# A decoder block on one NeuronCore: seven products of quarters also for the six gate segments and the way out, and one list of steps

## The chip, the core and the metric

The kernel runs on one core of a Trainium2 chip. The metric is the device time of one execution in microseconds; before the change the median of three runs is 2732.26 us (2726.07 to 2732.51).

## What is computed

The input `x` has 2048 tokens of 1024 columns, all in float32; there is one layer.

```python
h = rms_norm(x, norm_mix)
c_gate, b_gate, a_in, u, v, g_a, g_b = split(h @ w_in)      # w_in: 1024 x 7168, seven segments of 1024
y_a = b_gate * causal_depthwise_conv3(c_gate * a_in)
y_b = gelu(u) * (tril(W_s[head]) @ layer_norm(gelu(v)) + b) # within chunks of 128 tokens, 8 heads
merged = sigmoid(g_a) * y_a + sigmoid(g_b) * y_b
x = x + merged @ w_out                                      # 1024 x 1024
hid = square(relu(rms_norm(x, norm_mlp) @ w_ff1))           # 1024 x 4096
x = x + hid @ w_ff2                                         # 4096 x 1024
return rms_norm(x, final_norm)
```

## The kernel before, in words

Every float32 operand of a product is split into two fp32r parts (`split`, lines 105 to 107): ScalarE copies the high part, VectorE subtracts it to get the low one. A product of two such pairs is three matmuls on TensorE, high by high, high by low and low by high (`mm3`, lines 109 to 113; `passes`, line 684 for the feed-forward part). One matmul takes a 128 x 128 stationary tile and 512 moving columns and adds into one of eight PSUM banks.

The tokens come in two blocks of 1024. Each block goes through the mixer: the `v` segment (`v_half`, with the layer norm in `layer_norm` and the products with `W_s` in `sgu_mix`, lines 372 and 373), then the six segments C, A, B, U, GA, GB for each group of 128 columns (`turned_half`), and the way out (`out_pass`, by `natural_pass`; line 592 adds the products to the rows of x). These use plain products, all eight steps over the 1024 rows of the weights. The mixer keeps its operands in 36 slots of 128 x 1024 (`big`).

The feed-forward part is cut otherwise. The activations (tokens by columns) and the weights are each seen as four quarters, and sums of quarters make seven products of half size in each direction instead of eight. The products have names, 1 to 7, and run in the order of `ORDER`, "1627543". FF1 (`ff1_steps`) makes a step of each product of a pair of column tiles: 12 matmuls on one bank. The steps of neighbouring pairs are interleaved. FF2 (`ff2_steps`) makes a step of each row tile of a product: 12 matmuls over four banks, and eight such steps follow one another before the next product begins. Sums of quarters of the activations are made once and kept in HBM (`h2d`, `hidd`; `quarter_jobs` makes those of `h2d`: it loads rows of x1, normalizes them, turns them on TensorE at line 394 and sums them); sums of the weights are made on VectorE just before use (line 674 subtracts, line 671 adds), and the result is split (`split_new`).

In "1627543" the products 1 and 2 share a bank or set of banks, 6, 7 and 4 a second and 5 and 3 a third, so that two products on one set never follow one another directly, except within FF1's interleaving. A product's first use of a bank clears it and later ones add to it, and between them VectorE or ScalarE reads it.

`drive` (line 693) writes the order: before it runs step s it issues the loads of steps up to s + 8 (9 in FF2), and makes the operands (`prep`) of steps up to s + 4. TensorE and SyncE (SP, the queue of the loads) keep the order in which the program is written; the other engines' order is planned by priority, and loaded x rows and splits in the mixer carry a raised priority (`PRIO`). The feed-forward part has 5 buffers for split weights (`wunit`), 12 for raw loads (`rawq`) and 7 for held operands (`hold`). Between the mixer and the feed-forward part the pools are closed and others opened. GpSimd (POOL) computes the power -0.5 of the norms and issues the DMAs that write `x1d`, `h2d` and `hidd`.

Of the kernel before, what the change touches and what calls it, by code (L numbers as in the profile page):

```python
# [8 lines left out]
F32 = mybir.dt.float32  # L9
# [12 lines left out]
PRIO = 600  # L22
# [3 lines left out]
ORDER = "1627543"  # L26
C_SEG, B_SEG, A_SEG, U_SEG, V_SEG, GA_SEG, GB_SEG = range(7)


@with_exitstack  # L30
def hybrid_block_kernel(
# [29 lines left out]

    nc = tc.nc
# [4 lines left out]
    H = sgu_w.shape[1]  # L67

    const = ctx.enter_context(tc.tile_pool(name="const", bufs=1))
    stat = ctx.enter_context(tc.tile_pool(name="stat", bufs=8))  # L70
    psum = ctx.enter_context(tc.tile_pool(name="psum", bufs=8, space=bass.MemoryType.PSUM))
    mixer = ctx.enter_context(ExitStack())

    def mixer_pool(name, bufs):
        return mixer.enter_context(tc.tile_pool(name=name, bufs=bufs, reuse_waits="tile"))

    mconst = mixer_pool("mconst", 1)
    big = mixer_pool("big", 36)
    rawp = mixer_pool("rawp", 3)
    hlp = mixer_pool("hlp", 3)  # L80
    work = mixer_pool("work", 4)
    bcp = mixer_pool("bcp", 3)
# [10 lines left out]
    def pair(t):  # L93
        return t.rearrange("p (a b) -> p a b", a=2)
# [4 lines left out]
    def wk():  # L99
        return work.tile([P, HB], F32, tag="wk", name=nm("wk"))  # L100

# [3 lines left out]
    def split(hi, lo, src):  # L105
        nc.scalar.activation(hi, src, AF.Copy)  # L106
        nc.vector.tensor_tensor(lo, src, hi.bitcast(F32), ALU.subtract)  # L107

    def mm3(ps, stat_hl, mov_hl, first, last):
        (sh, sl), (mh, ml) = stat_hl, mov_hl  # L110
        nc.tensor.matmul(ps, lhsT=sh, rhs=mh, start=first, stop=False)  # L111
        nc.tensor.matmul(ps, lhsT=sh, rhs=ml, start=False, stop=False)  # L112
        nc.tensor.matmul(ps, lhsT=sl, rhs=mh, start=False, stop=last)  # L113


    def nat(w, r0, c0):
        return w[r0 : r0 + 2 * P, c0 : c0 + HB].rearrange("(k p) c -> p k c", p=P)

    def trn(w, c0):
        return w[:, c0 : c0 + P].rearrange("(k p) c -> p k c", p=P)  # L120

    def j_order(j):
        if j % 2 == 0:
            return (C_SEG, A_SEG, B_SEG, U_SEG, GA_SEG, GB_SEG)
        return (C_SEG, A_SEG, B_SEG, GA_SEG, GB_SEG, U_SEG)

    ORDER_AB = ((0, 0), (0, 1), (1, 0), (1, 1))

    def block_units():
        u = []  # L130
        for hf, h in ORDER_AB:
            u += [(("v", hf, h, q), nat(w_in, 2 * P * q, V_SEG * D + h * HB)) for q in range(4)]
        for j in range(KT):
            u += [(("in", seg, j), trn(w_in, seg * D + j * P)) for seg in j_order(j)]
        for hf, h in ORDER_AB:
            u += [(("o", hf, h, q), nat(w_out, 2 * P * q, h * HB)) for q in range(4)]
        return u

    units = [u for _ in range(NBLK) for u in block_units()]
    raws, hls = {}, {}  # L140
    loaded, ready, used = [0], [0], [0]

    def load_to(n):
        while loaded[0] < min(n, len(units)):
            i = loaded[0]
            t = rawp.tile([P, D], F32, tag="raw", name=nm("raw"))
            src = units[i][1]
            nc.sync.dma_start(out=t.rearrange("p (k c) -> p k c", k=src.shape[1]), in_=src)
            raws[i] = t
            loaded[0] += 1  # L150

    def ready_to(n):
        while ready[0] < min(n, len(units)):
            i = ready[0]
            load_to(i + 1)
            t = hlp.tile([P, 2, D], F32R, tag="hl", name=nm("hl"))
            with tc.high_priority(offset=PRIO):
                split(t[:, 0, :], t[:, 1, :], raws.pop(i))
            hls[i] = t
            ready[0] += 1  # L160

    def unit(key, ahead=2):

        i = used[0]
        assert units[i][0] == key, (units[i][0], key)
        used[0] += 1
        ready_to(i + 1 + ahead)
        load_to(i + 6)
        t = hls.pop(i)
        k = units[i][1].shape[1]  # L170
        return [
            (
                t[:, 0, :].rearrange("p (k c) -> p k c", k=k)[:, m, :],
                t[:, 1, :].rearrange("p (k c) -> p k c", k=k)[:, m, :],
            )
            for m in range(k)
        ]
# [4 lines left out]
    mhalf = const.tile([P, CH], F32, name="mhalf")  # L182
    nc.gpsimd.memset(mhalf, -0.5)
    junk = const.tile([P, D], BF16, name="junk")
    vecs = const.tile([P, 5 * KT], F32, name="vecs")
    sguT = mconst.tile([P, H, 2, P], F32R, name="sguT")
    zt = mconst.tile([P, 2 + BLK], F32, name="zt")
    tails = mconst.tile([P, KT, 2], F32, name="tails")


    x1d = [[tc.dram_tile([P, D], F32, name=f"x1d{b}_{i}") for i in range(2 * CH)] for b in range(NBLK)]
    h2d = [{p: tc.dram_tile([P, CH, HB], F32, name=f"h2d{b}_{p}") for p in ORDER} for b in range(NBLK)]
    hidd = [{p: tc.dram_tile([P, NPAIR, HB], F32, name=f"hidd{b}_{p}") for p in ORDER} for b in range(NBLK)]

    def vec(row, k):
        return vecs[:, row * KT + k : row * KT + k + 1]

# [841 lines left out]
```

## Time and profile before

| what | value |
|---|---|
| median of three runs | 2732.26 us |
| the profiled execution: time, span | 2727.57 us, 2725.9 us |
| TensorE busy (PE) | 2688.8 us, 99% |
| VectorE busy (DVE) | 1529.3 us, 56% |
| ScalarE busy (ACT) | 1035.4 us, 38% |
| GpSimd busy (POOL) | 205.3 us, 8% |
| mean granted TensorE clock | 0.995 of full |
| moved by DMA | 354.45 MB |

The profiled execution is one run; its span goes from the first to the last instruction. Busy time is the union of an engine's instructions, so that in a group of matmuls that overlap in the pipeline the mean duration is longer than the distance from one to the next.

### The profile page before, as it was taken

The numbers are of one execution on the slowest core, as the hardware profiler recorded it, in microseconds if no ns is written. First come the engines' busy times: TensorE is split into PE (matmuls) and PEld (weight loads), VectorE is DVE, ScalarE is ACT, GpSimd is POOL, SyncE is SP. The second block draws the span as 40 slices with busy tenths as digits, with TensorE's granted clock in tenths as the row PEclk, the third lists the DMA queues.
The fourth block names the chain that finished last, engine by engine and source line by source line (L and its number), as shares of the span: only waits on it lengthen the run. The fifth ranks groups of instructions, "written<-read, shape, count | busy, mean of one in ns | idle before, by whom it ended". The sixth has DMA issues, their size and how long they took to land.

```text
span 2725.9 us, 31946 instructions
## 1 busy us (share of the span) xinstructions
PE 2688.8 (99%) x12061; PEld 2231.1 (82%) x12061; DVE 1529.3 (56%) x2336; ACT 1035.4 (38%) x1668; POOL 205.3 (8%) x381
## 2 busy tenths in 40 slices
PE   9999999999999999999998999999999999999998
PEld 7888888888888888888876888878888888888886
DVE  5752233223456322232356877686667779686885
ACT  5422222222343121222223555565555444464444
POOL 0000000000000000000021323212122000010001
PEclk9999999999999999999998999999999999999999
DMA  5211111113631111111267756474446654482631
GB/s 198 73 45 48 47 47 54 47 47 132 218 115 55 39 55 47 47 48 53 67 254 250 230 198 207 159 247 155 143 166 241 234 183 140 139 296 95 215 108 62
DMA packets 275166, 354.45 MB, mean 130 GB/s; under 512 B 16540, under 2 KB 181444, under 8 KB 275012
## 3 DMA queue, kind: packets, MB, share of 16 engines
q1 hardware_dynamic: 245700, 262.21, 29.9%
q0 software_dynamic: 24704, 81.81, 8.0%
q10 hardware_dynamic: 4608, 8.39, 0.8%
q8 instruction: 95, 1.56, 0.2%
q14 instruction: 59, 0.48, 0.1%
HBM read 262.16 MB, written 90.18 MB: 129 GB/s over the span
## 4 chain that ended last, share of the span: by engine, by line
PE 95%; DMA 2%; issue 1%; DVE 1%; ACT 0%; POOL 0%; SPq 0%; POOLq 0%; ACTq 0%; DVEq 0%
PE ps L684 43%; PE ps L113 17%; PE ps L111 17%; PE ps L112 16%; DMA rq<-h2d 1%; PE ps L373 1%; PE ps L372 1%; DMA big<-x1d 1%; PE ps L267 1%; PE ps L394 0%; PE ps L453 0%; DVE hold L107 0%; DMA rq<-in_w_ff_dram 0%; ACT hold L106 0%; DVE r L671 0%
## 5 line engine op out<-in xcount | busy, mean ns | idle before, releaser
L684 PE MATMUL ps<-hold,wu 128*128 128x512 f32 x2688 | 617.7, 392 | 16.0 <-ACT wu L106 10.2
L684 PEld LDWEIGHTS ps<-hold,wu 128*128 128x128 f32 x2688 | 507.6, 189 | 124.4 <-ACT wu L106 10.6
L684 PE MATMUL ps<-wu,hold 128*128 128x512 f32 x2688 | 609.4, 389 | 0.0
L111 PE MATMUL ps<-big,hl 128*128 128x512 f32 x1536 | 597.7, 389 | 0.0
L113 PE MATMUL ps<-big,hl 128*128 128x512 f32 x1536 | 597.6, 389 | 0.0
L112 PE MATMUL ps<-big,hl 128*128 128x512 f32 x1536 | 597.6, 389 | 0.0
L684 PEld LDWEIGHTS ps<-wu,hold 128*128 128x128 f32 x2688 | 504.5, 188 | 104.8
L106 ACT ACTIVATE hl<-raw 128x1024 fp32r<-128x1024 f32 x160 | 169.5, 1060 | 707.8 <-PE ps L113 575.4
L107 DVE TENSOR_TENSOR hl<-raw,hl 128x1024 fp32r<-128x1024 f32 x160 | 195.7, 1223 | 388.7 <-ACT hl L106 388.4
L113 PEld LDWEIGHTS ps<-big,hl 128*128 128x128 f32 x1536 | 288.3, 188 | 60.0
L112 PEld LDWEIGHTS ps<-big,hl 128*128 128x128 f32 x1536 | 288.4, 188 | 59.8
L111 PEld LDWEIGHTS ps<-big,hl 128*128 128x128 f32 x1536 | 288.3, 188 | 59.3
L111 PE MATMUL ps<-hl,big 128*128 128x512 f32 x512 | 200.4, 391 | 0.0
L113 PE MATMUL ps<-hl,big 128*128 128x512 f32 x512 | 199.4, 389 | 0.0
L112 PE MATMUL ps<-hl,big 128*128 128x512 f32 x512 | 199.2, 389 | 0.0
L107 DVE TENSOR_TENSOR hold<-rq,hold 128x512 fp32r<-128x512 f32 x280 | 181.5, 683 | 11.3 <-ACT hold L106 11.2
L106 ACT ACTIVATE hold<-rq 128x512 fp32r<-128x512 f32 x280 | 157.7, 618 | 54.7 <-DMA rq<-h2d 38.7
L106 ACT ACTIVATE wu<-hold 128x512 fp32r<-128x512 f32 x160 | 100.1, 629 | 193.8 <-PE ps L684 192.0
L107 DVE TENSOR_TENSOR wu<-hold,wu 128x512 fp32r<-128x512 f32 x160 | 109.7, 688 | 102.0 <-ACT wu L106 101.9
L802 POOL DMA_DIRECT2D hidd<-r x224 | 122.0, 545 | 467.3 <-ACT r L749 294.0
L106 ACT ACTIVATE wu<-rq 128x512 fp32r<-128x512 f32 x160 | 100.1, 628 | 117.9 <-PE ps L684 117.5
L107 DVE TENSOR_TENSOR wu<-rq,wu 128x512 fp32r<-128x512 f32 x160 | 109.7, 687 | 56.5 <-ACT wu L106 56.5
(120 smaller groups left out, 2150.3 us busy)
## 6 DMA issues: line engine op xcount, KB each, us to landing
raw<-in_w_in_dram SPq DMA_DIRECT2D x128, 512.0 KB, 3.7
hidd<-r POOLq DMA_DIRECT2D x224, 256.0 KB, 2.8
rq<-hidd SPq DMA_DIRECT2D x224, 256.0 KB, 3.5
rq<-in_w_ff_dram SPq DMA_DIRECT2D x128, 256.0 KB, 3.1
hold<-in_w_ff_dram SPq DMA_DIRECT2D x64, 512.0 KB, 7.4
big<-in_x_dram SPq DMA_DIRECT2D x32, 512.0 KB, 8.0
raw<-in_w_out_dram SPq DMA_DIRECT2D x32, 512.0 KB, 3.4
rq<-h2d SPq DMA_DIRECT2D x56, 256.0 KB, 5.1
```

Source lines behind the costliest of these rows:

```text
L106: nc.scalar.activation(hi, src, AF.Copy)
L107: nc.vector.tensor_tensor(lo, src, hi.bitcast(F32), ALU.subtract)
L111: nc.tensor.matmul(ps, lhsT=sh, rhs=mh, start=first, stop=False)
L112: nc.tensor.matmul(ps, lhsT=sh, rhs=ml, start=False, stop=False)
L113: nc.tensor.matmul(ps, lhsT=sl, rhs=mh, start=False, stop=last)
L267: nc.tensor.transpose(ps[:, i * P : (i + 1) * P], t[:, k * P : (k + 1) * P], ident)
L372: nc.tensor.matmul(o, lhsT=hi[:, cs], rhs=r, start=True, stop=False)
L373: nc.tensor.matmul(o, lhsT=lo[:, cs], rhs=r, start=False, stop=True)
L684: nc.tensor.matmul(ps, lhsT=stat_of(a), rhs=mov_of(b), start=first and n == 0, stop=last and n == 2, skip_group_check=goes_on,)
L802: nc.gpsimd.dma_start(out=hidd[blk][p2][:, i, :], in_=src)
```

## The change

The way of the feed-forward part is taken to the six gate segments and to the way out, whose 5376 matmuls become 4704; the `v` segment keeps plain products. The mixer's own helpers (`unit`, `natural_pass`, `turned_half`, `mm3`) go. Every stage is now a list of steps, and one `drive` runs the ten stages v0, in0, v1, in1, out0, out1, FF1 (two blocks) and FF2 (two blocks) with loads 8 steps and operands 3 steps ahead. What passes between stages lies in HBM: the sums of the normalized x of the second block (`h1d`), the mixed heads (`mixd`, written in pieces of 128 x 128), the sums of the merged rows (`md`) beside those that were there. The new order "1674253" lets 1, 6, 7 and 4 add up in one bank, with a reading after each. The layer norm and the products with `W_s` go in between the steps as jobs, row by row, and so do the jobs that make sums of quarters. The gain and bias of the layer norm move behind the products with `W_s`; the bias takes 16 matmuls of 256 columns. One set of pools serves all stages; raised priorities are dropped.

```diff
-ORDER = "1627543"
+ORDER = "1674253"
+GROUP = {"1": "b", "6": "b", "7": "b", "4": "b", "2": "d", "5": "c", "3": "c"}
...
-    big = mixer_pool("big", 36)
-    rawp = mixer_pool("rawp", 3)
-    hlp = mixer_pool("hlp", 3)
...
+    hold = pool("hold", 1)
+    wunit = pool("wunit", 4)
+    rawq = pool("rawq", 9)
+    half = pool("half", 8)
+    big = pool("big", 12)
...
+    def pair_steps(hq, cols, sink):
...
+        def run(p):
+            first = p in "125"
+            if first:
+                st[GROUP[p]] = bank()
+            ps = st[GROUP[p]]
+            u, h = units.pop(p), hq[p]
+            for k in range(CH):
+                passes(
+                    ps,
+                    lambda a: u[:, a, k * P : (k + 1) * P],
+                    lambda b: h[:, b, k, :],
+                    first and k == 0,
+                    k == CH - 1,
+                    not first,
+                )
+            if p in "167":
+                st["s" + p] = hf()
+                copy(st["s" + p], ps)
+            else:
+                m, n = QUARTER[p]
+                sink(m, n, ps, {"2": st["s1"], "3": st["s6"], "5": st["s7"], "4": None}[p])
...
+        for i in range(CH):
+            jobs += [lambda i=i: norm(i), nothing, lambda i=i: mix(i, 0), lambda i=i: mix(i, 1)]
...
+            def b_sink(m, n, ps, a, st=st):
+                y = st["y"][n][:, tok(m)]
+                mul(y, y, plus(hf() if a is not None else None, ps, a))
...
+    def row_steps(a_src, w, rows_of, nk, i0, x1, places, finish):
...
             for r in range(CH):
                 passes(
-                    banks[group][r],
+                    banks[GROUP[p]][r],
                     lambda a: h[:, a, n % CH, r * P : (r + 1) * P],
                     lambda b: u[:, b, :],
                     first and n == 0,
-                    n == NK - 1,
+                    n == nk - 1,
                     not first,
                 )
-            if n < NK - 1:
+            if n < nk - 1:
                 return
             for r in range(CH):
...
+                m, c = {"1": (0, 0), "6": (0, 1), "7": (1, 1)}.get(p) or QUARTER[p]
+                t = x1[r + m * CH][:, c * HB : (c + 1) * HB]
+                add(t, banks[GROUP[p]][r], t)
+                if p not in "167":
+                    finish(r + m * CH, c)
...
+        spread(v, 17, 0.9, 16, lambda blk=blk: late[blk, 0])
+        spread(inn, 0, 0.8, 16, lambda blk=blk: late[blk, 1])
...
+    jobs = h2_jobs(0)
+    spread(outs[1], 1, 0.8, len(jobs), lambda jobs=jobs: jobs)
+    jobs2 = h2_jobs(1)
+    spread(ff1s[0], 16, 4, len(jobs2), lambda: jobs2)
+    for ph in outs + ff1s + [ff2_steps(blk, rotate("453")) for blk in blocks]:
+        phases += ph
...
+    drive(phases, 8, 3)
```

`spread(steps, n0, every, ...)` puts job i in front of step `int(n0 + i * every)`. The jobs of one row pair in `h2_jobs` are, in this order, load and normalize row r, turn it, load and normalize row r + 4, turn it, sum. `late[blk, m]` holds for each of four rows the norm, an empty job and two jobs of products with `W_s`.

## Rows read from the trace of the kernel before

**Rows 1.** Page, part 1: busy time, share of the span, instructions.

```profile
PE 2688.8 (99%) x12061; PEld 2231.1 (82%) x12061; DVE 1529.3 (56%) x2336; ACT 1035.4 (38%) x1668; POOL 205.3 (8%) x381
```

**Rows 2.** Page, part 4: the chain that ended last, by engine.

```profile
PE 95%; DMA 2%; issue 1%; DVE 1%; ACT 0%; POOL 0%; SPq 0%; POOLq 0%; ACTq 0%; DVEq 0%
```

**Rows 3.** Windows of start, FF1, FF2 and end: length, busy us (instructions) by engine, clock, DMA.

```profile
0.00:13.00 13.00, 8.93 (x27) 6.58 (x28) 4.52 (x11) 6.94 (x10) 3.38 (x14) 1.00 0.86 330
...
1810.00:2040.00 230.00, 230.00 (x1016) 190.41 (x1016) 159.50 (x251) 118.69 (x197) 45.40 (x84) 1.00 0.49 160
2101.00:2711.00 610.00, 610.00 (x2693) 505.11 (x2692) 473.29 (x800) 285.19 (x523) 15.04 (x18) 1.00 0.49 169
2711.00:2726.00 15.00, 1.83 (x9) 1.18 (x7) 7.10 (x16) 5.78 (x12) 3.65 (x4) 0.73 0.37 140
```

**Rows 4.** Timeline of PE where stages meet: start, us, work, idle before it.

```profile
1373.61 3.27 PE L394 MATMUL ps<-ident,big 128*128 128x128 f32 x16 [3.98 <-DVE st L249]
...
1474.04 5.20 PE L684 MATMUL ps<-hold,wu 128*128 128x512 f32 x12 [10.21 <-ACT wu L106]
...
1481.26 12.81 PE L684 MATMUL ps<-hold,wu 128*128 128x512 f32 x48 [0.55 <-DVE hold L107]
1494.86 5.52 PE L684 MATMUL ps<-hold,wu 128*128 128x512 f32 x23 [0.80 <-DVE hold L107]
...
1799.56 3.02 PE L684 MATMUL ps<-hold,wu 128*128 128x512 f32 x12 [0.88 <-ACT h L771]
1805.16 7.13 PE L684 MATMUL ps<-hold,wu 128*128 128x512 f32 x23 [2.58 <-DVE h L671]
```

**Rows 5.** Page, part 5: matmul groups of the mixer's three passes, one of each shape.

```profile
L111 PE MATMUL ps<-big,hl 128*128 128x512 f32 x1536 | 597.7, 389 | 0.0
...
L111 PE MATMUL ps<-hl,big 128*128 128x512 f32 x512 | 200.4, 391 | 0.0
```

**Rows 6.** The chain in order of time: start, us, what.

```profile
1524.87 1.75 PE ps L394 x16
1526.61 54.43 PE ps L684 x240
```

**Rows 7.** Groups by line and shape: count, busy us, mean ns of one, idle before.

```profile
L107 DVE TENSOR_TENSOR hold<-rq,hold 128x512 fp32r<-128x512 f32 x280 | 181.5, 683 | 11.3 <-ACT hold L106 11.2
L106 ACT ACTIVATE wu<-hold 128x512 fp32r<-128x512 f32 x160 | 100.1, 629 | 193.8 <-PE ps L684 192.0 <-DMA out_dram<-r 0.8 <-ACT r L991 0.7
...
L373 PE MATMUL ps<-sguT,big 128*128 128x256 f32 x128 | 31.2, 281 | 0.0
...
L107 DVE TENSOR_TENSOR big<-big,big 128x1024 fp32r<-128x1024 f32 x16 | 19.5, 1220 | 2.3 <-ACT big L106 2.3
...
L225 DVE TENSOR_TENSOR big<-big,wk 128x128 f32<-128x128 f32 x8 | 1.8, 282 | 0.0
```

**Rows 8.** Timeline of DVE in FF2: end of product 6, end of product 7.

```profile
2148.12 2.48 DVE L671 TENSOR_TENSOR r<-ps,r 128x512 f32<-128x512 f32 x4
...
2188.58 0.69 DVE L107 TENSOR_TENSOR wu<-hold,wu 128x512 fp32r<-128x512 f32 x1 [2.03 <-ACT wu L106]
2189.19 2.48 DVE L671 TENSOR_TENSOR r<-ps,r 128x512 f32<-128x512 f32 x4
```

**Rows 9.** DMAs: one chain piece (start, us), then issues: count, KB each, us to landing.

```profile
1462.25 3.06 DMA x1d<-big
...
x1d<-big POOLq DMA_DIRECT2D x16, 512.0 KB, 10.2
...
jr<-x1d SPq DMA_DIRECT2D x8, 512.0 KB, 5.9
```

**Rows 10.** Windows of 2 us after idle times, columns as in rows 3.

```profile
1474.00:1476.00 2.00, 1.96 (x5) 1.54 (x6) 1.41 (x3) 0.00 (x0) 0.00 (x0) 0.50 1.10 323
...
1798.00:1800.00 2.00, 1.12 (x6) 0.62 (x5) 1.97 (x4) 1.61 (x3) 1.08 (x2) 1.00 0.92 273
...
1806.00:1808.00 2.00, 2.00 (x7) 1.62 (x6) 2.00 (x4) 2.00 (x5) 0.00 (x0) 0.61 0.76 260
```

More of the change, by code (lines that the diff above doesn't have):

```diff
@@ L21 @@
 CH = HB // P
-PRIO = 600
 WARM = 20
@@ L139, in hybrid_block_kernel @@
[L139 to L174, printed above, removed]
-            )
-            for m in range(k)
-        ]
+    def held(place, dt=F32R):
+        shape = [P, 2, CH, HB] if dt == F32R else [P, CH, D]
+        return hold.tile(shape, dt, tag=f"hold{place}", name=nm("hold"))
@@ new lines, in add, with sub, mul, copy @@
+    def add(o, a, b):
+        nc.vector.tensor_tensor(o, a, b, ALU.add)
+    def sub(o, a, b):
+        nc.vector.tensor_tensor(o, a, b, ALU.subtract)
+    def mul(o, a, b):
+        nc.vector.tensor_tensor(o, a, b, ALU.mult)
+    def copy(o, a):
+        nc.scalar.activation(o, a, AF.Copy)
+    def split(h, l, src):
+        copy(h, src)
+        sub(l, src, h.bitcast(F32))
+    def split_new(src):
+        u = wtile()
+        split(u[:, 0, :], u[:, 1, :], src)
+        return u
+    def passes(ps, stat_of, mov_of, first, last, goes_on=False):
+        for n, (a, b) in enumerate(((0, 0), (0, 1), (1, 0))):
+            nc.tensor.matmul(
+                ps,
+                lhsT=stat_of(a),
+                rhs=mov_of(b),
+                start=first and n == 0,
+                stop=last and n == 2,
+                skip_group_check=goes_on,
+            )
@@ new lines, in quarters, with load, prep @@
+    def quarters(hq, src, p, place=None):
+        parts = []
+        def load():
+            for r in range(CH):
+                t = rq()
+                nc.sync.dma_start(out=t, in_=src[p][:, r, :])
+                parts.append(t)
+        def prep():
+            t = held(place or p)
+            for r, part in enumerate(parts):
+                tr = slice(r * P, (r + 1) * P)
+                split(t[:, 0, :, tr], t[:, 1, :, tr], part.rearrange("p (k t) -> p k t", k=CH))
+            hq[p] = t
+        return load, prep
@@ L209, in load_sgu, with stagger, plus @@
+    def stagger(pairs):
+        place = {}
+        for i, pr in enumerate(pairs):
+            for n, p in enumerate(ORDER):
+                place[7 * i + 2 * n + 1] = pr[p]
+        return [place[k] for k in sorted(place)]
+    def plus(t, ps, addend):
+        if addend is None:
+            return ps
+        add(t, ps, addend)
+        return t
+    sg = {}
     def load_sgu():
@@ L975, in finish, with ff2_steps @@
+    def ff2_steps(blk, nxt):
+        x1, fs = [None] * (2 * CH), {}
+        sums = {}
+        def finish(i, h):
+            if not sums:
+                sums["t"] = small(2 * CH)
+                sums["fin"] = slot()
+                nc.sync.dma_start(out=sums["fin"], in_=final_norm.partition_broadcast(P))
+            fin = sums["fin"]
             t = x1[i]
@@ new lines, in ff2_steps, with first_rows @@
+        steps[2]["before"].append(lambda: rows_in(x1, lambda i: x1d[blk][i]))
+        return steps
+    wz = wtile()
+    nc.vector.memset(wz.bitcast(F32), 0.0)
+    ps = bank()
+    for _ in range(WARM):
+        nc.tensor.matmul(ps, lhsT=wz[:, 0, :P], rhs=wz[:, 0, :], start=True, stop=True)
+    hqs = [{} for _ in blocks]
+    h0, first = hqs[0], {}
+    def first_rows(m):
+        t = held("67"[m], F32)
+        for i in range(CH):
+            r0 = m * HB + i * P
+            nc.sync.dma_start(out=t[:, i, :], in_=x[r0 : r0 + P, :])
+        first["rows", m] = t
```

1227 lines of the change are left out of this document (551 added, 676 removed).

## The prediction

> **What bounds the kernel now.** I read the page's busy shares first: TensorE works 2688.8 of 2725.9 us [rows 1]. The chain that ended last says the same, 95% of it is TensorE [rows 2]. So a change pays by what it takes out of TensorE's work, and costs what it adds to TensorE's idle time. The timeline of TensorE shows where the 37 us of idle lie: the start (first 13 us) and the end (last 15 us) [rows 3], and the places where stages meet [rows 4]. In between, in long windows, TensorE is busy for every microsecond, though VectorE is at 69% in FF1 and 78% in FF2 [rows 3]. That is the second thing to see: VectorE at nearly four fifths of the time did not hold TensorE up, with operands made four steps ahead.
>
> **What a matmul costs.** The mean of 389 ns in the groups is the way through the pipeline; the distance from one to the next is what counts: 240 in 54.43 us, 0.2268 us each [rows 6]. A step of 12 is 2.72 us, a pair of column tiles (7 steps) 19.05 us.
>
> **What is removed.** The mixer's matmuls are three passes of 1536 + 512 [rows 5], 6144; 768 of them are the `v` segment's, 5376 the six segments' and the way out's. Seven eighths of these are 4704, so 672 go: 672 x 0.2268 = 152.4 us. All of it is on the path, since TensorE is never waiting there.
>
> **What is added on TensorE.** 16 matmuls of 256 columns for the bias: at most 16 x 0.281 = 4.5 us [rows 7], at half the distance of 512 columns 1.8; I take 2. With every wait as before, the span would be 2725.9 - 152.4 + 2 = 2575.5 us.
>
> **Waits that go.** The old meetings of stages disappear with their pools. The transposes that waited 3.98 us then took 3.27 us instead of 1.75 [rows 4, 6]: 5.5. At the opening of FF1: 10.21 + 0.55 + 0.80 us of idle, and 12 and 48 matmuls that took 5.20 and 12.81 us instead of 2.72 and 10.89 [rows 4]: 16.0. Between the blocks of FF1: 0.88 + 2.58 idle and 23 matmuls in 7.13 instead of 5.22: 5.4. Together 26.9, so 2548.6 without them. Start and end I leave as they are: the same rows are loaded and normalized before the first product, the same rows end FF2.
>
> Idle time costs twice. After 10.21 us of idle the granted clock was 0.50 of full, the lower level, 1.2 GHz; after 2.58 us it was 0.61 on the mean of 2 us; after 0.88 us still 1.00 [rows 10]. The slow matmuls cost 4.4 us after the long wait and 1.9 after that of 2.58 [rows 4]. I add 1.9 to each wait of 2.5 to 5 us, 4.5 to a longer one, nothing to one under 1.
>
> **VectorE's own speed.** One addition of 512 columns lasts 683 ns [rows 7], four in a row take 2.48 us [rows 8], so 0.60 us each when it has a backlog. A pair in a gate segment asks 7 splits, 4 weight sums, 3 sums at the bank and 4 products, 18 x 0.60 = 10.8 us, and about 1.6 for the convolution and the sums at the end of a column group: 12.4 of 19.05, 65%. FF1 before had 69% without a wait, so the long middle of the gate stages costs nothing; ScalarE, at 0.63 us an instruction [rows 7] and some 13 a pair, is under half. If that cover were gone, each us per pair would cost 48.
>
> **New waits, one after the other.**
> (a) out1. The jobs that load row 0 of x1 and turn it both stand in front of step 1, while row 0 is finished in the last step of out0. From that addition on: 0.7 for it, about 1.3 to issue the write on POOL, 3.06 for the write, 0.6 to issue the load, 5.9 for the load [rows 9], about 3 for the norm (the wait of 3.98 in rows 4 is one whose row had already come): 14.6 us, of which about one step and the early start of the addition, 3.8, are covered. 11 us idle and 4.5 of slow matmuls: 15.5. Bounds: 6, if the copying is quicker, and 25, if the write takes its median of 10.2 [rows 9]. The eight loads of x stand before it on SP and wait for out0's slots; the loads of step 10 and later are queued behind, eight steps (22 us) ahead of need, so they don't make it worse.
> (b) Layer norm. At the start of each gate stage the rows of the second half are normalized one step before TensorE wants them. The nearest row is again the 3.98 us; here a subtraction and a split of 1024 columns (1.22 us on VectorE [rows 7], as much on ScalarE) come on top, one step is cover: 4.5 idle, 1.9 slow. Then four rows ask of VectorE 16 pieces of 128 columns each, at most 0.282 us [rows 7], and about 2.7 besides, some 6 us; 24 us beside 23 of the stage's own in 13 steps (35.4 us) plus three steps of lead: 3.5 short. So 10 each, 20 for both; in the `v` stages, where the first rows are ready earlier, 8. POOL's new writes (235 more issues) share its queue with the norms' powers; it was 8% busy [rows 1], I add nothing. Sum 28, bounds 4 and 60.
> (c) Banks in out and FF2. Now 1, 6, 7, 4 and then 5, 3 follow each other on the same four banks; TensorE may not write a bank until VectorE has read it. Before, the four additions stood behind the next unit's split [rows 8]; counted back from TensorE's end at 2712.8 us [rows 3] in products of eight steps, 21.77 us each, product 7 ended at 2190.2 and its additions began 1.0 us earlier, so that a successor on the same banks would hardly have waited; product 6, whose weight sums load VectorE most, ended at 2146.6 and its additions began 1.5 us later. That is the rule and the exception among FF2's ends; two of the four ends of product 6 were late so. Six sets (two out, four half FF2) of four hand-overs: 18 at 0.3, three late ones at about 2.3 + 1.9, and 6 for last ends, where row norms stand between the additions: 24. Bounds 4 and 70. The out stages, at 104 x 0.60 = 62 of 76 us, have less room than FF2.
> (d) At each start of interleaved pairs products 1, 6, 7, 4 meet on one bank with no other step between: 12 times about 0.9, like the 0.88 of a bank waiting for ScalarE's copy [rows 4]: 11. Bounds 3 and 30.
> (e) The two openings of FF1, with three steps of lead and 9 raw buffers in place of four and 12: 9 (before 16.0 and 5.4). Bounds 5 and 20.
> (f) Jobs that take four of the eight half buffers at once, and out1's overload (62 + 26 of jobs in 76 us, most of it inside the wait of a): 6. Bounds 0 and 20.
> Sum 15.5 + 28 + 24 + 11 + 9 + 6 = 93.5. Span 2548.6 + 93.5 = 2642; the profiled execution lies 1.7 us above its span, 2644, and the median of the runs shown 4.7 above that execution, part of which is spread between runs: I say **2646 us**.
>
> The traffic grows by the sums that pass through HBM, but the DMA engines were busy only about half of the time in FF1 and FF2 [rows 3]; I cost it at nothing, and if loads came late it would show as SP's waits.
>
> **Rivals.**
> *The waits are hidden.* The planner of the other engines knows TensorE's order and puts the readings of banks first, as it did at most ends above; then a to f fall towards their lower bounds, about 22 to 50: 2572 to 2605. For it: FF2 went 610 us without one wait. Against: a is a dependence, no order removes it. Chance 0.2.
> *VectorE becomes the bound in the new stages.* With a lead of three steps the peaks no longer fit: 8 us an out block, 10 more each at the four layer norms, 4 at each of the four products 6 of FF2: 16 + 40 + 16 = 72, giving about 2715. For it: its work rises from 56% to near 75% of the time. Chance 0.19.
> *Slower: the hand-overs of the bank inside the pairs.* In 80 pairs TensorE returns to one bank three times after only one other step, 240 hand-overs, 228 of them counted at nothing. If ScalarE's copy came late by 0.42 us on the mean, that is 96 us: 2740, slower than before; at 0.88 each it is some 200, 2845; with half of them late, 2745. Against it: between the bank being ready and the copy starting FF1 has a step of 2.72 us, and an instruction takes 0.63. A page speaks for it: the Trainium skill, "TensorE: Matmul & The Clock Gate", section "A second HAM failure mode: psum-queue depth-cycling", tells of a kernel that cycled through banks and whose short idle times between groups let the clock swing between its levels. In this trace an idle of 0.88 us left the clock at 1.00 [rows 10], which speaks against. Chance 0.08.
> *No gain*, a sum of these between 2724 and 2740: 0.03. That the 672 matmuls don't go is excluded by the loops.
>
> **Numbers.** The forecast's own range is 2610 to 2685, chance 0.5. The range that should hold 8 times in 10 takes in part of both neighbours: 2585 to 2720. Faster by over 0.3% (8 us, about what a measurement here can tell): 0.5 + 0.2 + 0.19 = 0.89; same 0.03; slower 0.08.
>
> **What would show it.** TensorE with 11405 instructions (12061 - 672 + 16) and some 120 us of idle and slow time; the largest single idle time at the start of out1, its chain running over x1d's write and load; idle of 4 to 5 us where a gate stage starts; the long middle of the gate stages without idle; waits of 1 to 4 us at product ends in FF2 and out, put down to VectorE's line that adds from banks. Wrong would be: idle in every pair (then the slower rival), VectorE above 90% in a stage with TensorE waiting for splits (the bound), or a start of out1 without a wait.

## The result, and the profile after

The changed kernel takes **2707.04 us** (median of four runs, 2705.39 to 2710.74), the kernel before, run on the same chip, 2730.99. The ratio is 0.9917 [0.9900 to 0.9934]: faster, by 24 us. That lies inside the wide range of the forecast (2585 to 2720), outside its own (2610 to 2685) and 61 us above its 2646. Of the 86 us that were forecast, less than a third came.

The profiled execution after lies in a span of 2704.3 us (2725.9 before). The page's busy shares, against [rows 1]:

```profile
PE 2578.5 (95%) x11405; PEld 2125.2 (79%) x11405; DVE 1923.7 (71%) x3229; ACT 1264.5 (47%) x2205; POOL 354.2 (13%) x628
```

TensorE has 11405 instructions, as worked out, and does 110 us less. But it is idle for 125.8 us of the span, where it was idle for 37.1. The page's share hides a second loss: slow matmuls count as busy. I summed (1 - granted clock) x busy time over windows of 2 us: 6.9 us before, 37.5 after. So the account is:

| us | before | after | change |
|---|---|---|---|
| span | 2725.9 | 2704.3 | -21.6 |
| idle of TensorE (span less busy) | 37.1 | 125.8 | +88.7 |
| lost to a lower clock | 6.9 | 37.5 | +30.6 |
| the rest: work at full clock | 2681.9 | 2541.0 | -140.9 |

The work came out nearly as forecast (-150.4). The waits grew by 119 us in place of 67. Where they lie is seen in windows of the trace after (the columns are those of [rows 3]):

```profile
760.00:1195.00 435.00, 435.00 (x1936) 360.79 (x1935) 304.18 (x472) 175.94 (x290) 31.00 (x57) 1.00 0.28 86
1285.00:1320.00 35.00, 10.22 (x40) 8.29 (x39) 19.10 (x32) 7.64 (x14) 4.40 (x8) 0.61 0.90 343
1320.00:1420.00 100.00, 86.95 (x384) 70.83 (x382) 77.21 (x130) 38.04 (x67) 23.34 (x36) 0.93 0.66 207
1420.00:1445.00 25.00, 15.27 (x47) 11.32 (x47) 17.04 (x28) 12.41 (x23) 2.14 (x4) 0.80 0.77 244
1745.00:1775.00 30.00, 20.86 (x76) 16.05 (x77) 23.75 (x38) 19.20 (x36) 3.80 (x7) 0.83 0.73 231
1775.00:2055.00 280.00, 280.00 (x1237) 231.86 (x1236) 173.59 (x267) 156.92 (x268) 55.96 (x103) 1.00 0.50 163
2415.00:2690.00 275.00, 275.00 (x1215) 227.61 (x1214) 195.84 (x330) 120.45 (x219) 4.26 (x4) 1.00 0.37 124
```

The long middles (first and last two rows) have no idle at all: 435 us of the second gate stage, 280 of FF1, 275 of FF2, at clock 1.00. Between them, in the other rows, the stages meet: out1 (1285 to 1420), FF1's two openings (from 1420 and from 1745). DMA is busiest there, 0.90 in the worst stretch. The waits of TensorE after, by who released it (engine, line waited for: us, times, longest):

```profile
PE ps L218 <- DVE big L201: 40.4, 8, 24.8
PE ps L140 <- ACT hf L126: 19.6, 12, 6.4
PE ps L428 <- ACT big L126: 18.8, 6, 7.4
PE ps L140 <- DVE big L117: 7.2, 5, 3.2
PE ps L140 <- ACT big L770: 6.6, 1, 6.6
```

The first line is the transposes of x1's rows in out1 (line 218), the third the layer norm before the products with `W_s` (line 428). The second and fifth are banks that wait for ScalarE to read them, in FF1 but for 4.6 us of the second, which lie in the gate stages. By place, idle and slow time together, beside the terms of the prediction:

| term | forecast, us | after, us |
|---|---|---|
| (a) out1, from 1285 | 15.5 | 46.0 |
| (b) layer norms, both blocks, with the bias | 28 | 41.0 |
| (e) two openings of FF1 | 9 | 27.1 |
| (c) banks in out0 and FF2 | 24 | 18.7 |
| (d) pair starts in the gate stages | 11 | at most 6.4 |

Of the 18.7 us of (c), 6.7 are waits for VectorE to read a bank, 6.4 are waits for operands that ScalarE or VectorE had not yet split, and most of the rest is slow matmuls.

The timeline of out1's start, with the one wait of 24.78 us:

```profile
1287.45 8.81 SPq L732 DMA_DIRECT2D big<-in_x_dram  x8
1290.71 2.40 POOL L748 DMA_DIRECT2D x1d<-big  x4 [12.35 <-DVE big L117]
1298.47 0.33 SPq L209 DMA_DIRECT2D big<-x1d  x1
1311.83 1.06 ACT L200 ACTIVATE junk<-big 128x1024 bf16<-128x1024 f32 x1 [15.31 <-DMA big<-x1d]
1314.65 1.97 PE L218 MATMUL ps<-ident,big 128*128 128x128 f32 x8 [24.78 <-DVE big L201]
```

The eight x rows of the next step are issued first (8.81 us for eight), then four writes of x1d, then the load of x1's row 0 at 1298.47; ScalarE starts on that row only at 1311.83, 13.4 us after its issue. My sum had 5.9.

### The profile page after: what moved, and what is told of

Its sections match the earlier page's. It is cut to its first block, busy times and chain, and to the rows that moved or that the text cites. A ratio compares the mean times of both kernels' runs of the same rounds, so it can differ in the third digit from the quotient of the medians.

```text
span 2704.3 us, 33392 instructions
## 1 busy us (share of the span) xinstructions
PE 2578.5 (95%) x11405; PEld 2125.2 (79%) x11405; DVE 1923.7 (71%) x3229; ACT 1264.5 (47%) x2205; POOL 354.2 (13%) x628
## 3 DMA queue, kind: packets, MB, share of 16 engines
q0 software_dynamic: 38576, 123.24, 13.1%
## 5 line engine op out<-in xcount | busy, mean ns | idle before, releaser
L140 PE MATMUL ps<-hold,wu 128*128 128x512 f32 x6720 | 1546.9, 392 | 30.3 <-ACT hf L126 19.6
L140 PEld LDWEIGHTS ps<-hold,wu 128*128 128x128 f32 x6720 | 1265.9, 189 | 300.4 <-ACT hf L126 25.0
L140 PE MATMUL ps<-wu,hold 128*128 128x512 f32 x4128 | 963.6, 394 | 13.1 <-DVE big L117 7.2
L140 PEld LDWEIGHTS ps<-wu,hold 128*128 128x128 f32 x4128 | 782.8, 191 | 181.4 <-ACT wu L126 5.4
L120 DVE TENSOR_TENSOR wu<-rq,wu 128x512 fp32r<-128x512 f32 x464 | 318.9, 689 | 173.2 <-ACT wu L126 171.0
L126 ACT ACTIVATE wu<-rq 128x512 fp32r<-128x512 f32 x464 | 290.3, 627 | 301.7 <-PE ps L140 167.0
L126 ACT ACTIVATE hf<-ps 128x512 f32<-128x512 f32 x240 | 143.2, 597 | 294.3 <-PE ps L140 290.6
L120 DVE TENSOR_TENSOR wu<-hf,wu 128x512 fp32r<-128x512 f32 x240 | 165.4, 689 | 160.1 <-ACT wu L126 159.4
L126 ACT ACTIVATE wu<-hf 128x512 fp32r<-128x512 f32 x240 | 150.8, 628 | 261.2 <-DVE hf L120 128.1
L783 POOL DMA_DIRECT2D hidd<-big x224 | 122.3, 546 | 458.8 <-ACT big L771 436.7
L123 DVE TENSOR_TENSOR big<-big,hf 128x512 f32<-128x512 f32 x120 | 82.6, 688 | 11.8 <-ACT hf L600 11.7
```

The source lines that it names most:

```text
L120: nc.vector.tensor_tensor(o, a, b, ALU.subtract)
L123: nc.vector.tensor_tensor(o, a, b, ALU.mult)
L126: nc.scalar.activation(o, a, AF.Copy)
L140: nc.tensor.matmul(ps, lhsT=stat_of(a), rhs=mov_of(b), start=first and n == 0, stop=last and n == 2, skip_group_check=goes_on,)
L783: nc.gpsimd.dma_start(out=hidd[blk][p][:, i, :], in_=src)
```

## The experiments

All start from the kernel after, and are compared with the kernel before on the same chip (median about 2730). The differences below are to 2707.04, the median after. Three causes were to be told apart for the wait in out1 (the dependence through x1d, the x rows that stand ahead, the order of the jobs), then the norm, then FF1's openings.

**The way through x1d (e1_source_x).** The jobs of block 0 take rows of x in place of x1 (FF1's input of that block then lacks the way out's additions).

```diff
-        return quarter_jobs(lambda i: x1d[blk][i], G_MLP, h2d[blk])
+        src = (lambda i: x[i*P:(i+1)*P, :]) if blk == 0 else (lambda i: x1d[blk][i])
+        return quarter_jobs(src, G_MLP, h2d[blk])
```

> The jobs of out1 that make the sums for FF1's first block take their rows from the input x instead of x1d, so the way from out0's last addition through HBM falls away; the additions of the way out are thereby left out of block 0's FF1 input. Theory 'dependence' (term a of the prediction: add, write, load, norm one after the other): the idle of 24.8 us before the first transposes of out1 falls below 5 us, and the time by 25 to 30 us, to about 2680. Theory 'queue' (the load stands behind eight loads of x rows and waits for their bandwidth): the load still lands 10 us or more after it is issued, the idle stays above 12 us, the time falls by 10 us or less.

Measured: 2705.8 (2702.74 to 2709.1), ratio 0.9909 [0.9893 to 0.9926], no difference to the kernel after. The timeline of its out1:

```profile
1299.50 0.33 SPq L209 DMA_DIRECT2D big<-in_x_dram  x1
1312.55 1.06 ACT L200 ACTIVATE junk<-big 128x1024 bf16<-128x1024 f32 x1 [15.73 <-DMA big<-in_x_dram]
1315.37 1.97 PE L218 MATMUL ps<-ident,big 128*128 128x128 f32 x8 [25.21 <-DVE big L201]
```

The row of x depends on no result, and the wait is the same 25 us: the load is not issued before 1299.5, behind the eight others on SP, and takes as long. But the edit leaves a second way to x1d open. The row needs a free slot, and the slots come free when rows of out0 have been written to x1d. SP's waits of this run between 1284 and 1301 us show it:

```profile
SPq L209 <- DMA x1d<-big: 2.9, 1, 2.9
```

So this run takes away the dependence of the data and not that of the slot, and it can't tell the dependence from the queue.

**The load ahead of the x rows (e2_loads_first).** The jobs that load x1's rows 0 and 1 go to the front of step 1, before the eight loads.

```diff
-    spread(outs[1], 1, 0.8, len(jobs), lambda jobs=jobs: jobs)
+    for i in range(len(jobs)):
+        if i in (0, 2):
+            outs[1][1]["before"].insert(i // 2, jobs[i])
+        else:
+            at(outs[1], int(1 + 0.8 * i), jobs[i])
```

> In out1 the loads and norms of rows 0 and 4 are put ahead of the eight loads of x rows in step 1; all else stands. Theory 'queue': row 0's load lands some 6 us after it is issued instead of 13, the first idle falls from 24.8 to 11 to 15 us, the time by 10 to 18 us, to about 2692; the x rows come later, so a wait of the first additions of out1 of a few us may take part of it back. Theory 'dependence': the idle stays above 20 us and the time within 4 us.

Measured: 2699.12 (2694.5 to 2700.02), ratio 0.9885 [0.987 to 0.99], 8 us faster, a little less than the 10 to 18 expected. The timeline:

```profile
1294.73 0.86 SPq L209 DMA_DIRECT2D big<-x1d  x2
1299.67 1.06 ACT L200 ACTIVATE junk<-big 128x1024 bf16<-128x1024 f32 x1 [5.31 <-DMA big<-x1d]
1302.89 1.97 PE L218 MATMUL ps<-ident,big 128*128 128x128 f32 x8 [14.43 <-DVE st L193]
```

Now the load is worked on 4.9 us after its issue, as I had it, and the wait falls to 14.43, nearer to the 11 of my sum. So of the 24.78 us the eight loads ahead make 10: the row was issued 3.7 us later (1298.47 against 1294.73) and took 8.5 longer (13.4 against 4.9). But the next long wait of the transposes grew from 3.68 to 5.47 us.

**Both (e12_both)**, the two edits together (it leaves out the same additions as e1_source_x): is what is left in e2 the way through x1d?

> As e1_source_x (rows from the input x instead of x1d for FF1's first block, so the additions of the way out are left out there) and as e2_loads_first (the loads of rows 0 and 4 ahead of the eight of x rows) at once. Each alone left 25.2 and 14.4 us of idle before out1's first transposes. If what e2 left is the way through x1d (term a), it goes here: idle 4 us or less, the time 8 to 14 us below e2's 2699. If it is the wait for a free slot (the slots are those of out0's rows, free only when x1d is written), the idle stays near 14 and the time near 2699.

Measured: 2693.35 (2689.97 to 2697.51), ratio 0.9872 [0.9855 to 0.9888]. The timeline:

```profile
1286.99 1.63 SPq L209 DMA_DIRECT2D big<-in_x_dram  x2
1289.57 11.77 SPq L732 DMA_DIRECT2D big<-in_x_dram  x8
1296.10 1.06 ACT L200 ACTIVATE junk<-big 128x1024 bf16<-128x1024 f32 x1 [0.97 <-DMA big<-in_x_dram]
1299.30 1.97 PE L218 MATMUL ps<-ident,big 128*128 128x128 f32 x8 [11.02 <-DVE big L201]
```

Here the rows of x find free slots, and the eight loads are the ones that wait for x1d. Issued 7.7 us sooner than in e2, the row is worked on only 3.6 us sooner: its load now takes 9.1 us where e2's took 4.9, though it stands ahead of the eight here too. Without both ways through x1d the wait is 3.4 us shorter, and the time is 6 us below e2's, between what the two theories expect. Why the load takes longer is not shown; DMA moves x1d's writes and eight loads in the same stretch.

**Room between load and transposes (e3_gaps).** TensorE keeps the written order, and the job that turns row 0 stands in the same step as the one that loads it. Here each pair of rows is loaded some four steps before it is turned:

```diff
-    spread(outs[1], 1, 0.8, len(jobs), lambda jobs=jobs: jobs)
+    for i, n in enumerate((1, 5, 1, 5, 6, 6, 9, 6, 9, 10, 10, 13, 10, 13, 14, 14, 17, 14, 17, 18)):
+        at(outs[1], n, jobs[i])
```

> In out1 the jobs stand as before in number and order of rows, but each load and norm is put four steps before the transposes that need it, and both rows of a pair together. Theory 'latency' (a load and the transposes of it in front of one step or of neighbours leave TensorE to wait for the load): the first idle falls by the cover of four steps, 24.8 to about 14, the four later ones of 0.9 to 4.3 us (12.6 together) go, fewer slow matmuls follow; the time falls by 22 to 32 us, to about 2680. Rival 'VectorE is full in out1' (88 us of work in 76): the idle only moves to other steps, the time stays within 6 us.

Measured: 2686.16 (2683.25 to 2689.95), ratio 0.9842 [0.9827 to 0.9856], 21 us faster, where the theory had 22 to 32 and the rival at most 6. TensorE's timeline in out1:

```profile
1284.74 14.67 PE L140 MATMUL ps<-wu,hold 128*128 128x512 f32 x64
1303.14 3.67 PE L140 MATMUL ps<-wu,hold 128*128 128x512 f32 x9 [3.73 <-DVE big L117]
...
1316.85 3.34 PE L218 MATMUL ps<-ident,big 128*128 128x128 f32 x16 [7.96 <-DVE st L193]
```

64 matmuls run where 22 ran, then a second wait shows that had lain under the first: VectorE's additions (line 117) lack the x rows, so the banks stay full. That is 3.73 + 1.13, and 7.96 remain at the transposes. The later steps of out1 still wait 10.4 us (13.1 before), most of it for such additions.

**The x rows in two halves as well (e5_out1).** e3's order, and the second four x rows one step later for block 1.

```diff
-        steps[1]["before"].append(
-            lambda: rows_in(x1, lambda i: x[r0 + i * P : r0 + (i + 1) * P, :])
-        )
+        src = lambda i: x[r0 + i * P : r0 + (i + 1) * P, :]
+        steps[1]["before"].append(lambda: rows_in(x1, src, range(CH)))
+        steps[LATE[blk]]["before"].append(lambda: rows_in(x1, src, range(CH, 2 * CH)))
```

> As e3_gaps, and out1's eight loads of x rows are parted: four stand in front of step 1, ahead of the loads of rows 0 and 4 of x1, the other four in front of step 2, behind them (out0's likewise). Theory 'queue' (row 0's load of x1 waits behind 4 MB of x rows, not for x1d): the row's load is issued and lands some 5 us earlier than in e3_gaps, the idle at out1's start (3.7 + 1.1 + 8.0 us there) falls to 5 or less, the time by 5 to 10 us against e3_gaps, to about 2678. If the queue does not matter, the time stays at 2686 within 3.

Measured: 2683.12 (2678.43 to 2684.87), ratio 0.9838 [0.9821 to 0.9856]; the intervals of e3 and e5 overlap, so only the traces tell them apart. TensorE's waits in the same place are 3.53, 0.22, 0.81 and 2.42 us, 7.0 in place of 12.8. The theory had 5 or less, and a time 5 to 10 us lower where 3 came: it is borne out in part.

```profile
1300.82 2.10 PE L140 MATMUL ps<-wu,hold 128*128 128x512 f32 x6 [3.53 <-DVE big L117]
1309.68 4.05 PE L218 MATMUL ps<-ident,big 128*128 128x128 f32 x16 [2.42 <-DVE big L201]
```

**The products with `W_s` one job later (e4_norm_sooner).** In the kernel after, a row's `mix` (its products with `W_s`) begins two jobs behind its `norm`; here it begins three behind. The next row's `norm` stays in its job, which it now shares with the second `mix` of the row before.

```diff
-        jobs = []
+        jobs = [nothing] * 17
...
-            jobs += [lambda i=i: norm(i), nothing, lambda i=i: mix(i, 0), lambda i=i: mix(i, 1)]
+            jobs[4 * i + 3] = lambda i=i: mix(i, 0)
+            jobs[4 * i + 4] = lambda i=i: (mix(i, 1), norm(i + 1) if i + 1 < CH else None)
+        jobs[0] = lambda: norm(0)
```

> In all four layer-norm stretches the products with W_s of a row come one job later (three instead of two after its norm), and the next row's norm stays where it was. Theory 'latency' (norm, split and transposed products follow too closely): the idle of 25 us before the products with W_s falls to 10 or less, with some 4 us fewer lost to the low clock; the time falls by 12 to 20 us, to about 2690. Rival 'VectorE is full there' (term b's second part): the idle stays above 18 us, the time within 5 us.

Measured: 2692.75 (2690.87 to 2694.98), ratio 0.9865 [0.9851 to 0.988], 14 us faster. In the kernel after, TensorE waited at 46 (the bias), 81, 113, 142, 684 and 739 us. Besides the bias, one long place stays in each block, 4.68 + 1.39 us at 679 and this one in TensorE's timeline:

```profile
110.58 0.58 PE L428 MATMUL ps<-big,big 128*128 128x256 f32 x1 [4.73 <-ACT big L126]
111.84 1.86 PE L428 MATMUL ps<-big,big 128*128 128x256 f32 x7 [0.68 <-DVE big L120]
...
117.87 1.10 PE L428 MATMUL ps<-big,big 128*128 128x256 f32 x8
```

That is the first row of the second half, whose norm can't begin before the `v` stage's last sums. The idle time before line 428 fell from 25.0 to 17.7 us, where the theory had 10 or less and the rival above 18; with the slow matmuls, (b) lost 13 of its 41 us. So about a third of (b) was distance between two jobs. What makes the rest is not shown, and VectorE's speed is not excluded there.

**FF1's openings.** Five runs. Two more raw buffers (e7_rawq11):

```diff
-    rawq = pool("rawq", 9)
+    rawq = pool("rawq", 11)
-    big = pool("big", 12)
+    big = pool("big", 11)
```

> 11 raw buffers instead of 9, paid for with one slot (11 instead of 12). Theory 'buffers' (at FF1's two openings the quarters' 28 loads go through nine buffers, and ScalarE's splits wait for them with the copies of the banks behind): the idle of some 20 us at the two openings falls to 12 or less, the time by 6 to 12 us, to about 2698. Rival 'bandwidth' (the loads take the DMA engines' time): the openings stay as they are, the time within 4 us, or higher by what the missing slot costs.

Measured: 2703.43 (2697.32 to 2708.74), ratio 0.9903 [0.9884 to 0.9922], no difference in the time. The trace does differ: the first opening costs 8.3 us of idle and slow time in place of 13.9 (11.8 to 16.0 in the other runs with nine buffers and all loads), the second 15.4 in place of 13.1, and FF2, with the end of FF1, 20.4 in place of 15.2. So the buffers have a part in the first opening; whether the missing slot takes the gain back was not tried. A lead of two steps (e8_lead2, `drive(phases, 8, 2)`) and of four (e9_lead4, `drive(phases, 8, 4)` with `wunit` 5 and `big` 11):

> Operands are made two steps ahead instead of three, with all buffers as they are. If the lead of three steps is what holds TensorE up (term e and the rival 'VectorE becomes the bound' of the prediction), two make it worse by 30 us or more, to 2737 or above, with idle inside the long gate stages. If three is ample but for the openings, the time rises by 10 us or less.

> Operands four steps ahead and five buffers for split weights, as the kernel before had in its feed-forward part, paid for with one slot (11). If the shorter lead is what the openings, the layer-norm starts and the ends of products lost, the time falls by 15 us or more, to 2692 or below. If the lead is no matter, the time stays within 5 us, or rises by what the missing slot costs.

Measured: 2700.43 (2695.82 to 2702.37), ratio 0.9897 [0.9881 to 0.9913], and 2694.75 (2693.62 to 2695.44), ratio 0.9878 [0.9863 to 0.9894]. The shorter lead isn't slower. The longer one gains 12 us, between what the two theories expect, but FF1's openings still wait 5.90 + 1.85 + 2.38 and 5.05 + 2.35 + 0.69 + 1.13 us. Its gain lies elsewhere: idle and slow time fell from 9.0 to 1.0 us in the first gate stage (200 to 660) and from 15.2 to 6.7 in FF2 with the end of FF1. The lead and the fifth weight buffer were not tried apart. Then block 1's held operands made earlier, within FF1's first block (e10_opening):

```diff
-            bring(ff1s[blk][(0, 1, 2, 3, 4, 6, 8)[n]], *quarters(hqs[blk], h2d[blk], p))
+            k = ((0, 1, 2, 3, 4, 6, 8), (-5, -3, -1, 1, 2, 4, 6))[blk][n]
+            target = ff1s[blk] if k >= 0 else ff1s[blk - 1]
+            bring(target[k], *quarters(hqs[blk], h2d[blk], p))
```

> Only the second opening of FF1: the quarters of the second block are loaded and split one to five steps earlier (each as early as its held buffer can come free), the first opening stays. Theory 'order' (ScalarE's splits of quarters, which wait for their loads, stand before the copies and Relu that free banks, so work that is spread out stops the wait): the idle around 1744 to 1776 us (10.2, and 3.0 of slow matmuls) falls to 5 or less in all, the time by 7 to 11 us, to about 2698, the first opening unchanged at 9 to 10 us of idle. Rival 'bandwidth' (9 MB of quarters and weights in some 40 us): the idle only moves to before the opening, the time stays within 3 us.

Measured: 2705.39 (2701.26 to 2705.97), ratio 0.9913 [0.9898 to 0.9928], and the second opening's idle and slow time 12.1 in place of 13.2: no difference, the theory falls. A cause can be read from the timeline of ScalarE and TensorE at the first opening, in the kernel after:

```profile
1417.26 2.88 PE L140 MATMUL ps<-hold,wu 128*128 128x512 f32 x12
...
1423.23 0.63 ACT L126 ACTIVATE hold<-rq 128x512 fp32r<-128x512 f32 x1 [1.37 <-DMA rq<-h2d]
...
1424.70 1.27 ACT L126 ACTIVATE hold<-rq 128x512 fp32r<-128x512 f32 x2 [0.83 <-DMA rq<-h2d]
...
1425.88 0.58 ACT L126 ACTIVATE hf<-ps 128x512 f32<-128x512 f32 x1
...
1426.51 5.49 PE L140 MATMUL ps<-hold,wu 128*128 128x512 f32 x12 [6.37 <-ACT hf L126]
```

The bank is full at 1420.1; its copy (`hf<-ps`) needs 0.58 us and starts at 1425.88, because on ScalarE the splits of held operands (`hold<-rq`) stand ahead of it, and some of these wait for their loads. Of the 5.7 us ScalarE waits 2.2 and splits in the rest. If the late loads are the cause, fewer loads must end it, with the splits as many as before (e13_one_load: each held operand of FF1 loads one of its four pieces and splits it four times, so three quarters of FF1's held operands are not those of the computation):

```diff
-            for r in range(CH):
+            for r in range(loads):
...
-            for r, part in enumerate(parts):
+            for r in range(CH):
+                part = parts[r % loads]
```

> Leaves out three of the four loads of each held operand of FF1 (28 operands in all, 14 per block half as large again in traffic as the weights there): the one piece that is loaded is split four times, so the splits of ScalarE and VectorE and all matmuls are as many as before, and only 21 of the 28 loads of 256 KB at each opening go. After the change the two openings cost 9.7 + 4.2 and 10.2 + 3.0 us of idle and slow time, 27.1 together, and in the first the copies out of the banks stand on ScalarE behind splits that wait 1 to 3 us each for these loads. Theory 'late loads hold ScalarE's queue': with a quarter of the loads the splits never wait, the copies come in time, and the openings fall under 8 us together: about 2687 us (2683 to 2692). Rival 'work': 4 copies and 4 subtractions for each held operand, beside the weights' own, are too much for the first steps whatever the loads do: openings stay above 18, 2698 to 2707. In between, 2692 to 2698, both have a part.

(There are 14 such operands, seven for each block, with 28 loads at each opening.) Measured: 2688.62 (2685.88 to 2693.17), ratio 0.9851 [0.9834 to 0.9867], 18 us faster, as the theory had it. The openings' idle and slow time fell from 27.1 to 11.1 us (the theory had under 8, the rival above 18); the other stretches stayed within a few us of what they were. What is left is the same thing once more, in ScalarE's and TensorE's timeline of this run:

```profile
1421.74 0.63 ACT L126 ACTIVATE hold<-rq 128x512 fp32r<-128x512 f32 x1 [2.30 <-DMA rq<-h2d]
1422.28 0.58 ACT L126 ACTIVATE hf<-ps 128x512 f32<-128x512 f32 x1
```

```profile
1422.91 3.02 PE L140 MATMUL ps<-hold,wu 128*128 128x512 f32 x12 [2.99 <-ACT hf L126]
```

So late loads that hold ScalarE's queue make the larger part of (e). Whether they are late by the DMA engines (0.77 busy there) or by SP's waits for free buffers isn't settled. Two more buffers took 5.6 us off the first opening (e7), and SP's waits of the kernel after between 1400 and 1440 us are mostly for buffers that VectorE's part of a held operand's split sets free:

```profile
SPq L266 <- DVE hold L120: 14.7, 13, 2.7
```

**All that helped, together (e11_all).** e5, e4 and e10, and the last held operands of block 1's `v` stage brought 15 steps sooner (`v[7 + 3 * n]` for `v[22 + 3 * n]`).

> The parts together: out1's jobs four steps apart with its x rows in two halves (as e5_out1), the products with W_s one job later (as e4_norm_sooner), the second opening of FF1 earlier (as e10_opening), and in the second block's v stage the quarters 6, 7 and 5 from steps 7, 10 and 13 on instead of 22, 25 and 28, out of the layer norm's way. If the losses are separate waits, as the ledger of idle times says, the gains add: 24 + 14 + 9 + 4 = 51 us below 2707, about 2656. If VectorE's or ScalarE's total work is what is paid in one place or another, the sum comes to less than half of that, above 2680.

Measured: **2662.63** (2658.35 to 2666.86), ratio 0.976 [0.9745 to 0.9774]: faster than both kernels, 44 us under the one after. The page's busy shares and TensorE's waits:

```profile
PE 2565.3 (97%) x11405; PEld 2112.9 (80%) x11405; DVE 1921.3 (72%) x3229; ACT 1264.2 (48%) x2205; POOL 348.5 (13%) x628
```

```profile
PE ps L140 <- DVE big L117: 21.8, 7, 6.3
PE ps L140 <- ACT hf L126: 21.3, 13, 8.7
PE ps L218 <- DVE big L201: 9.6, 7, 3.0
PE ps L428 <- ACT big L126: 6.4, 2, 4.7
```

As many instructions on every engine, 34.5 us less idle (91.3) and 15.8 less slow time (21.7). The waits at the transposes fell from 40.4 to 9.6, at the norm from 18.8 to 6.4; the banks that wait for ScalarE (21.3) are as they were, the second opening among them, whose loads e10's edit moves without gain. The waits for VectorE's additions rose from 7.2 to 21.8: 8.9 of these lie in out1, where the additions lack x rows, and 6.3 at FF1's second opening, whose first wait was put down to ScalarE before. The parts' own gains, 24 (e5) and 14 (e4), add up. The rest of the 44 points to the moved operands of block 1's `v` stage, which were not run alone: around that block's layer norm (640 to 760 us) idle and slow time fell to 2.9 us, where e4 alone left 11.6 of 18.4.

## Why the prediction was right and wrong

**Right:** the sign and its reason. The 672 matmuls went, TensorE's work at full clock fell by 140.9 us of the 150.4 forecast, and the long middles have no wait. VectorE is at 70% in the second gate stage and TensorE never waits there, so the rival of VectorE as the bound is out for the long stages, and a lead of two steps cost nothing (e8). Its number, 2715, came nearer than mine, but by other ways: most of the loss lies in out1, at the layer norms and in FF1's openings. In FF2 it may have a part, where 4.3 us are waits for weights not yet split and the longer lead with a fifth buffer brought a gain (e9).

The slower rival is out too: late readings inside the pairs were to cost 96 us or more, and the 435 us of the second gate stage show no idle, at clock 1.00. Outside the pair starts and FF1's openings TensorE waited for a copy out of a bank at 308, 409, 490 and 1593 us only, 0.40 + 1.95 + 0.91 + 1.49 us (the first three are in the table's 6.4 for (d)). At 409 the copy lacked a half buffer, which a write of `h1d` held: that is (f). At the other three it stood behind the square of a row that waited for its load, as here, in ScalarE's timeline of the kernel after:

```profile
488.01 1.06 ACT L200 ACTIVATE junk<-big 128x1024 bf16<-128x1024 f32 x1 [2.23 <-DMA big<-in_x_dram]
...
489.06 0.58 ACT L126 ACTIVATE hf<-ps 128x512 f32<-128x512 f32 x1
```

The Trainium skill ("TensorE: Matmul & The Clock Gate", section "A second HAM failure mode: psum-queue depth-cycling") tells of a clock that swings with short idle times between groups that cycle through banks. In the long middles no such idle arose; at FF1's first opening, where TensorE waited 6.37 and 2.67 us for copies out of a bank, the clock was 0.80 from 1420 to 1445. The waits were hidden, as the rival of hidden waits had it, in part of (d) and (c) only.

**The 9.5 us of work** that are missing are not explained by a run. Small groups of matmuls are not it: in e4 a group of eight starts at 117.87 and the next product at 118.81, 0.118 us a matmul of 256 columns, and before the change 16 in a row took 0.119 each. What fits is the number of waits, 52 in the kernel after and 10 before. A row of TensorE's timeline after:

```profile
1759.59 3.01 PE L140 MATMUL ps<-hold,wu 128*128 128x512 f32 x12 [0.69 <-ACT hf L126]
```

Twelve matmuls between two waits are busy for 3.01 us, at clock 1.00, where a step in a stream takes 2.72. At 0.29 for each of the 42 waits more, that would be 12 us; it is an estimate.

**Failed, step (a): "so they don't make it worse".** It measured 46.0 for 15.5, above its bound of 25. I looked for what the eight loads of x delay behind them, found the loads of step 10 in time, and didn't count that the load of x1's row itself is behind them: 10 of the 24.78 us (e2). I had also costed the traffic at nothing, on a mean of half the time, where in this stretch DMA is busy 0.90. And I counted one wait where the jobs of every later pair of rows wait again (13.1 idle and 5.7 slow after the first). The sentence "a is a dependence, no order removes it" was wrong: an order removes 12 of its 25 us (e3), 18 with the x rows in halves (e5). What the dependence alone costs stays open: e1 leaves that of the slots, and without both the wait is 3.4 us shorter than in e2 (e12).

**Failed, term (e):** 9 against 27.1. I took the opening from the lead and the number of buffers. The lead doesn't decide it (e8, e9), and the buffers have a part in the first opening only (e7). The larger part is that 28 loads come at once, and that on ScalarE, which must also read the banks, the splits that lack them stand ahead of the reading (e13: 11.1 left of 27.1). The bound of 20 was too low as well.

**Mis-sized, term (b):** 28 against 41, the bias' wait (1.72 + 0.88 idle and its slow matmuls) in it, which I had not counted at all. The first part of its mechanism was right: rows are late by the distance between `norm` and `mix` (e4 gives 13 back). The second, that VectorE is 3.5 us short in each stretch, is neither shown nor excluded.

**Near, but in part by luck, term (c):** 18.7 for 24, where only 6.7 us of idle are the hand-overs of banks that the sum counts.

**Mis-sized, the clock.** I charged 1.9 us to a wait of 2.5 to 5 and nothing to one under 1, as single idles in [rows 10] allowed. The terms name 14.0 us of slow matmuls (4.5 in (a), twice 1.9 in (b), three times 1.9 in (c)), and 7.8 were to go with the old meetings; measured, the loss grew by 30.6. Short waits can count: after 1.72 and 0.88 us at the bias, with one matmul between them, the clock went to the lower level. Windows of the kernel after:

```profile
44.00:46.00 2.00, 0.38 (x1) 0.19 (x1) 1.30 (x3) 1.54 (x2) 0.00 (x0) 1.00 0.31 70
46.00:48.00 2.00, 1.15 (x5) 1.15 (x6) 0.90 (x2) 0.00 (x0) 0.00 (x0) 0.56 0.59 193
48.00:50.00 2.00, 2.00 (x11) 2.00 (x10) 1.57 (x5) 0.00 (x0) 0.00 (x0) 0.50 0.00 0
50.00:52.00 2.00, 2.00 (x7) 1.61 (x7) 1.26 (x4) 0.00 (x0) 0.15 (x1) 0.50 0.00 0
52.00:54.00 2.00, 2.00 (x8) 1.65 (x7) 0.00 (x0) 0.00 (x0) 0.38 (x1) 0.74 0.54 219
...
1768.00:1770.00 2.00, 1.34 (x6) 1.12 (x7) 1.69 (x4) 2.00 (x5) 0.00 (x0) 1.00 0.09 32
```

TensorE is busy without a gap from 48 on and still runs at 0.50 until 52: about 3 us lost to 2.6 of idle, so this wait costs double. Not every wait does: 1.59 us before 1764.20 and 1.44 before 1768.66, with 12 matmuls between them, left the clock at 1.00 (last row).

## What to carry to other kernels

When a change merges stages, the price is at the meetings: write down for each queue (SP's loads, ScalarE's instructions) what the late item stands behind, not only what it depends on; here instructions that in part waited for loads held back a bank's reading of 0.58 us for 5.7. Use the DMA share of the stretch in question, not of the stage, before a load is given its usual duration. Cost the slow matmuls after a wait too: as much again as the idle at the bias, 5.7 for the 13.1 us of out1's later waits, 37.5 for 125.8 over this kernel.

## What was not expected of the hardware

A load of 512 KB landed in 4.9 to 5.9 us where it was issued ahead of the eight others (e2), and in 10.4 to 13.3 where it was issued behind them, on the same queue (the kernel after). Its place in the queue is not all of it: in e12, ahead of the eight as well, it landed in 9.1 to 10.8. And the hand-overs between TensorE and ScalarE on one bank, 240 in the gate stages and FF1, cost 4.8 us outside the pair starts and FF1's openings, where the slower rival had put 96 to 200.
